# The state scan of an S5 layer: from one block split between VectorE and GpSimd to pieces set between the gates' matrix products, all on VectorE

## The chip, the cores and the metric

The kernel runs on one core of a Trainium2 chip. The metric is the device time of one execution in microseconds (us); the time of a kernel is the median of several runs. A core has a matrix engine (PE, with its weight loads shown apart as PEld), a vector engine (DVE, VectorE), an activation engine (ACT, ScalarE), a general engine (POOL, GpSimd) and a queue that issues transfers (SP). Each engine works through its own instructions in an order that is fixed when the program is built.

## The reference, cut to what matters

The program is a two-layer decoder trunk of width 1024 over 2048 tokens. Its even layer has two branches; the change lies in branch B, a diagonal state space model with 32 groups of 16 channels and a complex state of 64 numbers for each group:

```python
proj = h @ even_w_in[i]
q, k, v, z_a, u, z_b = jnp.split(proj, [...], axis=-1)
o_a = stick_breaking_attention(q, k, v) * jax.nn.silu(z_a)
o_b = s5_mixer(u, ...) * jax.nn.silu(z_b)
x = x + jnp.concatenate([o_a, o_b], axis=-1) @ even_w_out[i]

def s5_mixer(u, ...):
    bu = einsum('gnp,blgp->blgn', b_bar, uf)                  # complex
    h  = associative_scan over time of  h_t = lam_bar * h_{t-1} + bu_t
    y  = Re(einsum('gpn,blgn->blgp', c, h)) + d_skip * uf
    y  = gelu(y);  return y * sigmoid(y @ w_glu + b_glu)
```

## The kernel before, in words

**Stages of the even layer.** `tile_trunk` (line 1233) calls in this order: `first_gates` and a first `gates` (half of z_a), `s5_in` (line 1278: the input u, its products with B, and the scan), a second `gates` (line 1279: the other half of z_a), `s5_out` (line 1280: the outputs from the state), a third `gates` (line 1283: z_b), then the GLU and the attention.

**The state.** Time is cut into 256 columns of eight tokens (`NC` = 256), so the recurrence runs over columns. The state tile has 128 partitions (a pair of groups, 64 states each), sixteen pairs, real and imaginary part, and 256 columns after one column of zeros. Before the change there are two such tiles, `H[0]` and `H[1]`, of eight pairs each, with the parts outermost: `[P, 2, 8, 257]`.

**`s5_in` (line 465).** For each half `cb` of the channels and each half of the time it makes eight products `j` of 24 matmuls (L67 to L69, tile `ups`): the activations hT, taken at every eighth token, are split into a rounded part on ACT (`sh`, L314) and a remainder on DVE (`sl`, L315). ACT copies the result to `U` (L487). Then four groups of transposes (`tp`, L491), ACT copies (`us`, L493) and products with B (`bp`, L500) follow, and DVE copies each `bp` into H (L504).

**The scan.** The scan over columns is a tree. `scan_up` (line 510) combines, for four pairs at a time, neighbouring columns at distance 1 (level 0, in two halves), 2 (level 1) and 4 (level 2) on DVE, and then walks a chain over every eighth column on POOL: 31 links of four small instructions for each tile (L530 to L533). `scan_down` (line 536) hands the results back through levels 2, 1 and 0 on DVE. One level step is `cplx_acc` (line 450), five DVE instructions: a product with the real factor into `ca` (L458), two products with the imaginary factor into `cb` (L460), their sum (L461) and the sum onto H (L462). The factors are `pwr` and `pwi`, made in `s5_setup` (line 213) by repeated squaring, one set for each level. `ca`, `cb` and the chain's `sa`, `sb` lie in the pools of `s5_in`, on the same side of the memory on which `s5_out` opens its own pools later.

**`gates` (line 420).** It loads eight pieces of a weight (split into `whi` on ACT and `wlo` on DVE) and, for each of four blocks `m` of 512 tokens, splits the activations (four `sh` on ACT, four `sl` on DVE), runs 96 matmuls into four accumulators `gps`, and hands them out (`silu_out`: a sigmoid on ACT, L364, a product on DVE, L365, a store). The four accumulators are reused from block to block, so a block can begin in an accumulator only when DVE's product L365 has read the one before. For `m` = 0 and 3 the loop over the weight's pieces is outermost; for 1 and 2 the loop over the four output slices is.

**`s5_out` (line 549).** For each quarter `ct` of the pairs it loads K0, Co and U, multiplies H by Co (L570) and U by K0 (L573) into `yps`, and makes the gelu on ACT and DVE (L577 to L582).

**What sets the order.** Nobody writes the order of an engine's queue by hand here. A scheduler (asked for in line 1370) plays the program through and gives each engine, whenever it is free, the instruction that comes first in the program text among those whose inputs and buffers are there. A piece of work that comes earlier in the text goes first wherever it is ready, and later work fills the gaps. The order it finds is then fixed, and on the chip an engine that reaches an instruction whose input is missing waits, with all that stands behind it.

Of the kernel before, what the change touches and what calls it, by code (L numbers as in the profile page):

```python
# [9 lines left out]
F32 = mybir.dt.float32  # L10
F32R = mybir.dt.float32r
BF16 = mybir.dt.bfloat16
AF = mybir.ActivationFunctionType
ALU = mybir.AluOpType
# [3 lines left out]
P = 128  # L18
L = 2048
D = 1024  # L20
# [92 lines left out]
NI = 16  # L113
NC = L // T8
# [41 lines left out]
def s5_setup(e, room, lr, li, dt, sn, sh, b_re, b_im, c_re, c_im, dsk, bin_d, k0_d, co_d):  # L156
# [10 lines left out]
    e.pwr = [e.cst.tile([P, NI], F32, name=f"pwr{a}") for a in range(4)]  # L167
    e.pwi = [e.cst.tile([P, 2, NI], F32, name=f"pwi{a}") for a in range(4)]
    with e.pool("s5s", 1, "right") as s, e.pool("s5t", 2, "right") as s2, e.pool("s5w", 1, "right") as sw, \
# [43 lines left out]
        for a in range(6):  # L213
# [206 lines left out]
def gates(e, pn, hT, w, c0, out_d, row0, lo_eng, between=None, also=None, ws=None, sp=None, last=LAST):  # L420
# [5 lines left out]
    for m in range(4):  # L426
# [11 lines left out]
        for f, k in order:  # L438
            wh, wl = ws[k]
            hi, lo = sp[k // 2]  # L440
            c = slice(f * P, f * P + P)
            i = mm3(nc, pss[f], wh[:, c], wl[:, c], hi[:, k % 2], lo[:, k % 2], k == 0,
                    k == (last[-1] if m == 3 else KD - 1))
# [6 lines left out]
def cplx_acc(e, tp, dst, src, lv, n, eng):  # L450

    nI = dst.shape[2]
    i0 = e.i0
# [10 lines left out]

def s5_in(e, pn, hT, w_in, bin_d, u_d, H, lo_eng):

    nc, tc = e.nc, e.tc
    with e.pool("u_b", 2, "right") as ub, e.pool("u_1", 1, "right") as u1, e.pool("u_p", 2, "right", PSUM) as up:
        ws = pn.load(w_in, 4 * D, 512, lo_eng)
        for cb in range(2):  # L470
            nc.vector.memset(H[cb][:, :, :, 0:1], 0.0)
# [3 lines left out]
            for half in range(2):  # L475
                U = ub.tile([P, 16, T8, 16], F32, tag="U", name="U")
                for j in range(T8):
# [9 lines left out]
                    nc.scalar.activation(U[:, :, j, :], ps.rearrange("c (g p) -> c g p", p=16), AF.Copy)  # L487
                for g4 in range(4):
# [14 lines left out]
                    i0 = g4 * 2  # L503
                    nc.vector.tensor_copy(H[cb][:, :, i0:i0 + 2, 1 + half * P:1 + (half + 1) * P], bp)  # L504
            scan_up(e, H[cb], cb * 8, u1, ub)
        for cb in range(2):
            scan_down(e, H[cb], cb * 8, u1)


def scan_up(e, H, i1, tp, t2):  # L510

    B = H[:, :, :, 1:]
    V, G = e.nc.vector, e.nc.gpsimd
    for i0 in range(0, 8, 4):
        e.i0 = i1 + i0
        b = B[:, :, i0:i0 + 4]
        for h in range(2):
            c = slice(h * 128, h * 128 + 128)
            bh = b[:, :, :, c]
            cplx_acc(e, tp, bh[:, :, :, 1::2], bh[:, :, :, 0::2], 0, 64, V)  # L520
        cplx_acc(e, tp, b[:, :, :, 3::4], b[:, :, :, 1::4], 1, 64, V)
        cplx_acc(e, tp, b[:, :, :, 7::8], b[:, :, :, 3::8], 2, 32, V)
    ii = slice(i1, i1 + 8)
    pr = e.pwr[3][:, ii].unsqueeze(1).to_broadcast([P, 2, 8])
    pi = e.pwi[3][:, :, ii]
    for c in range(15, NC, 8):
        src = B[:, :, :, c - 8]
        a = t2.tile([P, 2, 8], F32, tag="sa", name="sa")
        b = t2.tile([P, 2, 8], F32, tag="sb", name="sb")
        G.tensor_tensor(a, src, pr, ALU.mult)  # L530
        G.tensor_tensor(b, src[:, ::-1], pi, ALU.mult)
        G.tensor_tensor(a, a, b, ALU.add)
        G.tensor_tensor(B[:, :, :, c], B[:, :, :, c], a, ALU.add)  # L533


def scan_down(e, H, i1, tp):

    B = H[:, :, :, 1:]
    V = e.nc.vector
    for i0 in range(0, 8, 4):  # L540
        e.i0 = i1 + i0
        b = B[:, :, i0:i0 + 4]
        cplx_acc(e, tp, b[:, :, :, 11::8], b[:, :, :, 7:NC - 1:8], 2, 31, V)
        cplx_acc(e, tp, b[:, :, :, 5::4], b[:, :, :, 3:NC - 1:4], 1, 63, V)
        cplx_acc(e, tp, b[:, :, :, 2:128:2], b[:, :, :, 1:127:2], 0, 63, V)
        cplx_acc(e, tp, b[:, :, :, 128::2], b[:, :, :, 127:NC - 1:2], 0, 64, V)
# [827 lines left out]
```

## Time and profile before

| | |
|---|---|
| median of 3 runs | 2875.68 us (2871.69 to 2877.24) |
| the profiled execution, its own time | 2872.48 us |
| its span, first to last instruction | 2870.8 us |
| PE busy | 2765.3 us (96%) |
| DVE busy | 1719.9 us (60%) |
| ACT busy | 1365.0 us (48%) |
| POOL busy | 1197.6 us (42%) |
| mean granted clock of PE | 0.989 |

Shares of the whole span say little about a stage that takes a tenth of it. In the stage of the scan, from about 227 to 417 us of the span, DVE is the busiest engine beside PE, and the questions are where PE stands idle and what it waits for. The profile names for every idle stretch the instruction that ended it ("[16.98 <-DVE sg L365]"), and the timeline of the engine named shows what stood ahead of that instruction.

### The profile page before, as it was taken

To read this page: it belongs to the slowest core of one execution; us is meant where nothing else is said; L and a number is where in the kernel's file an instruction comes from. 1 tells how busy PE (TensorE), PEld (TensorE's weight loads), DVE (VectorE), ACT (ScalarE), POOL (GpSimd) and SP (SyncE) were. 2 spreads that over 40 slices of the span, in tenths; PEclk is the share of its full clock that TensorE was granted. 3 is DMA by queue.
4 is the path that set the end of the run, shared out by engine and by line. 5 is a ranking of instruction groups with operands and counts; after the bars stand their busy time and mean duration, and the time that the engine had idled before them with its cause. 6 is when DMAs were issued, how large, how long until landed. Compare 5 with 4: busy or idle time off the path is not lost.

```text
span 2870.8 us, 46525 instructions
## 1 busy us (share of the span) xinstructions
PE 2765.3 (96%) x17433; PEld 2496.6 (87%) x17433; DVE 1719.9 (60%) x2733; ACT 1365.0 (48%) x2988; POOL 1197.6 (42%) x1321
## 2 busy tenths in 40 slices
PE   6989979899999999999999999999999999999999
PEld 6788767889999999999899978887788999999887
DVE  7768965657676857685767783223345566565521
ACT  4576224446555655555555552223345566565310
POOL 7201821366665665666556730000023455455300
PEclk9999989999999999999999999999999999999999
DMA  5532136511110111111112124332131021121343
GB/s 170 153 81 75 58 94 201 173 44 43 29 41 27 45 29 40 29 41 27 41 27 73 58 72 143 104 103 86 56 99 41 31 67 54 36 78 60 125 137 114
DMA packets 246898, 215.69 MB, mean 75 GB/s; under 512 B 46256, under 2 KB 215568, under 8 KB 246160
## 3 DMA queue, kind: packets, MB, share of 16 engines
q1 hardware_dynamic: 246096, 210.62, 24.2%
q8 instruction: 137, 2.24, 0.3%
q10 hardware_dynamic: 576, 2.10, 0.2%
q14 instruction: 89, 0.73, 0.1%
HBM read 129.36 MB, written 74.65 MB: 71 GB/s over the span
## 4 chain that ended last, share of the span: by engine, by line
PE 78%; DVE 7%; POOL 4%; issue 4%; ACT 3%; DMA 3%; SPq 1%; ACTq 0%; POOLq 0%; DVEq 0%
PE av L807 6%; PE pp L68 6%; PE pp L67 6%; PE pp L69 6%; PE ops L69 5%; PE ops L68 5%; PE ops L67 5%; PE w L796 4%; PE gps L67 3%; PE gps L68 3%; PE gps L69 3%; PE qk L67 2%; PE qk L69 2%; PE qk L68 2%; PE z L68 2%
## 5 line engine op out<-in xcount | busy, mean ns | idle before, releaser
L719 POOL TENSOR_TENSOR sl<-hT,sh 128x1024 fp32r<-128x1024 f32 x128 | 322.2, 2518 | 343.0 <-ACT sh L718 304.8
L67 PE MATMUL pp<-whi,sh 128*128 128x384 f32 x1024 | 357.4, 349 | 0.7 <-ACT whi L314 0.6
L68 PE MATMUL pp<-wlo,sh 128*128 128x384 f32 x1024 | 351.1, 343 | 0.2
L69 PE MATMUL pp<-whi,sl 128*128 128x384 f32 x1024 | 348.0, 340 | 0.0
L790 DVE TENSOR_TENSOR_SCAN pt<-om,pt,zero 128x513 f32<-128x513 f32 x192 | 279.2, 1477 | 38.0 <-ACT om L788 37.3
L67 PE MATMUL gps<-sh,whi 128*128 128x512 f32 (+1 forms) x672 | 252.8, 389 | 23.1 <-DVE sg L365 20.3
L68 PE MATMUL gps<-sl,whi 128*128 128x512 f32 (+1 forms) x672 | 259.1, 386 | 3.5 <-DVE sl L315 3.5
L69 PE MATMUL gps<-sh,wlo 128*128 128x512 f32 (+1 forms) x672 | 256.5, 384 | 0.0
L799 DVE TENSOR_TENSOR tl<-w,th 128x512 fp32r<-128x512 f32 (+2 forms) x320 | 186.6, 599 | 95.5 <-ACT th L798 93.6
L798 ACT ACTIVATE th<-w 128x512 fp32r<-128x512 f32 (+2 forms) x320 | 163.9, 535 | 149.3 <-PE w L796 148.8
L315 DVE TENSOR_TENSOR sl<-hT,sh 128x1024 fp32r<-128x1024 f32 (+1 forms) x148 | 172.1, 1186 | 50.4 <-ACT sh L314 48.2
L69 PE MATMUL ops<-woh,ol 128*128 128x512 f32 x496 | 196.8, 397 | 0.7 <-DVE ol L315 0.7
L68 PEld LDWEIGHTS pp<-wlo,sh 128*128 128x128 f32 x1024 | 193.6, 189 | 3.8 <-POOL wlo L315 1.7
L67 PEld LDWEIGHTS pp<-whi,sh 128*128 128x128 f32 x1024 | 193.5, 189 | 3.6 <-ACT whi L314 1.3
L68 PE MATMUL ops<-wol,oh 128*128 128x512 f32 x496 | 196.2, 395 | 0.0
L67 PE MATMUL ops<-woh,oh 128*128 128x512 f32 x496 | 195.6, 395 | 0.0
L69 PEld LDWEIGHTS pp<-whi,sl 128*128 128x128 f32 x1024 | 193.3, 189 | 2.6
L790 DVE TENSOR_TENSOR_SCAN pt<-om,zero 128x129 f32<-128x129 f32 (+3 forms) x128 | 158.8, 1262 | 56.8 <-ACT om L788 56.2
L314 ACT ACTIVATE sh<-hT 128x1024 fp32r<-128x1024 f32 (+1 forms) x148 | 155.8, 1093 | 62.0 <-PE gps L69 32.5
L788 ACT ACTIVATE om<-z 128x512 f32<-128x512 f32 (+2 forms) x320 | 167.0, 538 | 37.6 <-PE z L784 22.7
L718 ACT ACTIVATE sh<-hT 128x1024 fp32r<-128x1024 f32 x128 | 135.5, 1059 | 90.8 <-PE pp L68 90.5
L796 PE MATMUL w<-ident,pt 128*128 128x128 f32 x1088 | 165.2, 273 | 8.6 <-DVE tl L799 6.0
(327 smaller groups left out, 8001.7 us busy)
## 6 DMA issues: line engine op xcount, KB each, us to landing
zs_d<-sg SPq DMA_DIRECT2D x80, 256.0 KB
o<-o_d SPq DMA_DIRECT2D x80, 256.0 KB
xt<-in_x_dram SPq DMA_DIRECT2D x28, 512.0 KB
r<-in_even_w_in_dram SPq DMA_DIRECT2D x64, 192.0 KB
zs<-zs_d SPq DMA_DIRECT2D x64, 128.0 KB
o_d<-ot SPq DMA_DIRECT2D x64, 128.0 KB
r<-in_odd_w_in_dram SPq DMA_DIRECT2D x64, 128.0 KB
zs<-zs_d SPq DMA_DIRECT2D x32, 256.0 KB
```

Source lines behind the costliest of these rows:

```text
L67: nc.tensor.matmul(out, lhsT=lhi, rhs=rhi, start=start, stop=False)
L68: nc.tensor.matmul(out, lhsT=lhi, rhs=rlo, start=False, stop=False)
L69: return nc.tensor.matmul(out, lhsT=llo, rhs=rhi, start=False, stop=stop)
L314: a = nc.scalar.activation(hi, src, AF.Copy)
L315: b = lo_eng.tensor_tensor(lo, src, hi.bitcast(F32), ALU.subtract)
L719: a = nc.gpsimd.tensor_tensor(sl, ht, sh.bitcast(F32), ALU.subtract)
L788: nc.scalar.activation(o[:, lo:512], z[:, :n], AF.Sigmoid, scale=-scale)
L790: nc.vector.tensor_tensor_scan(pt[:, lo:][:, ::-1], o[:, lo:][:, ::-1], zr.to_broadcast([P, n + 1]), 1.0 if prev[i] is None else prev[i], ...
L796: nc.tensor.transpose(w[:, s, :], pt[:, lo + s * P:lo + (s + 1) * P], e.ident)
L798: nc.scalar.activation(th[:, :ni, qs], w[:, :ni, :], AF.Copy)
L799: nc.vector.tensor_tensor(tl[:, :ni, qs], w[:, :ni, :], th[:, :ni, qs].bitcast(F32), ALU.subtract)
L807: nc.tensor.matmul(av[:, qs], lhsT=a[:, s, :], rhs=b[:, s, qs], start=diag and x == 0, stop=c == 0 and x == len(prods) - 1)
```

## The change

The arithmetic of the tree stays, but its last step up, its order and its engines change:

- One tile H holds all sixteen pairs, with the pair outermost: `[P, 16, 2, 257]`. ACT, not DVE, copies `bp` into it.
- The tree gets one more level (distance 8, level 3) in both directions, so the chain runs over every sixteenth column: 15 links instead of 31, each over all sixteen pairs at once, four instructions of 128x32 on DVE instead of POOL. One more power of the factor is made for it (seven squarings instead of six, 5 sets of `pwr` and `pwi`).
- Levels 0 and 1 are made pair by pair with fused instructions (`cplx_pair`): one `scalar_tensor_tensor` for the product with the real factor and its sum onto H, and one each for the two parts of the product with the imaginary factor, three instructions of one pair over all its columns and without temporary tiles. Levels 2 and 3 keep `cplx_acc`, over eight pairs at once.
- The scan becomes a list of pieces. A piece is one pair of level 0 or 1, one `cplx_acc`, or one link. `s5_in` runs one piece behind every product `j`; as the list is empty during the first half of the channels, that is 16 of the 18 pieces up of the first eight pairs, during the second half. What is left (2 + 18 pieces up, 15 links, 36 pieces down) is run from the second `gates`, in front of every eighth product of three matmuls, that is four times for each block `m`: six pieces each time, four within the chain. By the counts that gives 24 pieces in block 0 (2 + 18 up and 4 links), 18 in block 1 (11 links, 7 down), 24 in block 2 (all down) and the last 5 in block 3.
- The temporary tiles lie in a pool of their own (`Ht`); the pool of `y` in `s5_out` has two buffers instead of three.

```diff
@@ s5_setup
-    e.pwr = [e.cst.tile([P, NI], F32, name=f"pwr{a}") for a in range(4)]
-    e.pwi = [e.cst.tile([P, 2, NI], F32, name=f"pwi{a}") for a in range(4)]
+    e.pwr = [e.cst.tile([P, NI], F32, name=f"pwr{a}") for a in range(5)]
+    e.pwi = [e.cst.tile([P, 2, NI], F32, name=f"pwi{a}") for a in range(5)]
...
-        for a in range(6):
+        for a in range(7):
@@ gates
-        for f, k in order:
+        for n, (f, k) in enumerate(order):
+            if slot is not None and n % 8 == 7:
+                slot(m, n // 8)
@@
+def cplx_pair(e, dst, src, lv, i):
+
+    V, MU, AD = e.nc.vector, ALU.mult, ALU.add
+    V.scalar_tensor_tensor(dst, src, e.pwr[lv][:, i:i + 1], dst, MU, AD)
+    for r in range(2):
+        V.scalar_tensor_tensor(dst[:, r], src[:, 1 - r], e.pwi[lv][:, r, i:i + 1], dst[:, r], MU, AD)
+
+class Scan:
+    def __init__(self, e, H, tp):
+        self.e, self.H, self.tp, self.todo = e, H, tp, []
+
+    def level(self, cb, lv, dst, src):
+        B = self.H.rearrange("p i r c -> p r i c")[:, :, :, 1:]
+        if lv < 2:
+            for i in range(cb * 8, cb * 8 + 8):
+                self.todo.append(lambda i=i: cplx_pair(self.e, B[:, :, i, dst], B[:, :, i, src], lv, i))
+        else:
+            i0, i = cb * 8, slice(cb * 8, cb * 8 + 8)
+            self.todo.append(lambda: cplx_acc(self.e, self.tp, B[:, :, i, dst], B[:, :, i, src], lv, i0,
+                                              self.e.nc.vector))
+
+    def up(self, cb):
+        for lv in range(4):
+            s = 2 << lv
+            self.level(cb, lv, slice(s - 1, NC, s), slice(s // 2 - 1, NC, s))
+
+    def down(self, cb):
+        for lv in range(3, -1, -1):
+            s = 2 << lv
+            self.level(cb, lv, slice(s + s // 2 - 1, NC, s), slice(s - 1, NC - 1, s))
+
+    def chain(self):
+        self.todo += [lambda c=c: self.link(c) for c in range(31, NC, 16)]
+
+    def link(self, c):
+        e, B, G = self.e, self.H.rearrange("p i r c -> p r i c")[:, :, :, 1:], self.e.nc.vector
+        src = B[:, :, :, c - 16]
+        a = self.tp.tile([P, 2, NI], F32, tag="sa", name="sa")
+        b = self.tp.tile([P, 2, NI], F32, tag="sb", name="sb")
+        G.tensor_tensor(a, src, e.pwr[4].unsqueeze(1).to_broadcast([P, 2, NI]), ALU.mult)
+        G.tensor_tensor(b, src[:, ::-1], e.pwi[4], ALU.mult)
+        G.tensor_tensor(a, a, b, ALU.add)
+        G.tensor_tensor(B[:, :, :, c], B[:, :, :, c], a, ALU.add)
+
+    def run(self, n):
+        for f in self.todo[:n]:
+            f()
+        del self.todo[:n]
@@ s5_in
                     nc.scalar.activation(U[:, :, j, :], ps.rearrange("c (g p) -> c g p", p=16), AF.Copy)
+                    sc.run(1)
...
-                    nc.vector.tensor_copy(H[cb][:, :, i0:i0 + 2, 1 + half * P:1 + (half + 1) * P], bp)
-            scan_up(e, H[cb], cb * 8, u1, ub)
-        for cb in range(2):
-            scan_down(e, H[cb], cb * 8, u1)
+                    i0 = cb * 8 + g4 * 2
+                    nc.scalar.activation(H[:, i0:i0 + 2, :, 1 + half * P:1 + (half + 1) * P],
+                                         bp.rearrange("p a i c -> p i a c"), AF.Copy)
+            sc.up(cb)
@@ s5_out
-    ... e.pool("so_3", 3, "right") as s3
+    ... e.pool("so_3", 2, "right") as s3
...
-                                             rhs=H[ct // 2][q, a, ct % 2 * 4 + i, 0:NC], start=a == 0, stop=False)
+                                             rhs=H[q, ct * 4 + i, a, 0:NC], start=a == 0, stop=False)
@@ tile_trunk
-        H = [hpool.tile([P, 2, 8, NC + 1], F32, name=f"H{cb}") for cb in range(2)]
-        s5_in(e, pn, hT, w0, bin_d, u_d, H, V)
-        gates(e, pn, hT, w0, 3 * D + 512, zs_d, 512, V)
+        H = hpool.tile([P, NI, 2, NC + 1], F32, name="H")
+        scan = Scan(e, H, sr.enter_context(e.pool("Ht", 1, "right")))
+        s5_in(e, pn, hT, w0, bin_d, u_d, H, scan, V)
+        n_up = len(scan.todo)
+        scan.chain()
+        n_chain = len(scan.todo) - n_up
+        scan.down(0)
+        scan.down(1)
+
+        def slot(m, i):
+            scan.run(4 if n_down < len(scan.todo) <= n_down + n_chain else 6)
+
+        n_down = len(scan.todo) - n_up - n_chain
+        gates(e, pn, hT, w0, 3 * D + 512, zs_d, 512, V, slot=slot)
+        scan.run(len(scan.todo))
         s5_out(e, H, u_d, k0_d, co_d, y_d)
```

More of the change, by code (lines that the diff above doesn't have):

```diff
@@ L417, in first_gates, with gates @@
     return ws, angles, rows[:, 3]
-def gates(e, pn, hT, w, c0, out_d, row0, lo_eng, between=None, also=None, ws=None, sp=None, last=LAST):
+def gates(e, pn, hT, w, c0, out_d, row0, lo_eng, between=None, also=None, ws=None, sp=None, last=LAST,
+          slot=None):
     nc = e.nc
@@ L447, in gates, with cplx_acc @@
     return out
-def cplx_acc(e, tp, dst, src, lv, n, eng):
-    nI = dst.shape[2]
-    i0 = e.i0
+def cplx_acc(e, tp, dst, src, lv, i0, eng):
+    nI, n = dst.shape[2:]
     a = tp.tile([P, 2, nI, n], F32, tag="ca", name="ca")
@@ L462, in cplx_acc, with s5_in @@
     eng.tensor_tensor(dst, dst, a, ALU.add)
-def s5_in(e, pn, hT, w_in, bin_d, u_d, H, lo_eng):
+def cplx_pair(e, dst, src, lv, i):
[38 more added lines that the diff above has]
+        del self.todo[:n]
+def s5_in(e, pn, hT, w_in, bin_d, u_d, H, sc, lo_eng):
     nc, tc = e.nc, e.tc
@@ L469, in s5_in @@
         ws = pn.load(w_in, 4 * D, 512, lo_eng)
+        nc.vector.memset(H[:, :, :, 0:1], 0.0)
         for cb in range(2):
-            nc.vector.memset(H[cb][:, :, :, 0:1], 0.0)
             bt = u1.tile([P, 2, 8, P], F32, tag="bt", name="bt")
@@ L502, in s5_in @@
                                                  rhs=us[:, i * 2 + par, :], start=True, stop=True)
-                    i0 = g4 * 2
-                    nc.vector.tensor_copy(H[cb][:, :, i0:i0 + 2, 1 + half * P:1 + (half + 1) * P], bp)
-            scan_up(e, H[cb], cb * 8, u1, ub)
-        for cb in range(2):
-            scan_down(e, H[cb], cb * 8, u1)
[L510 to L546, printed above, removed]
+                    i0 = cb * 8 + g4 * 2
+                    nc.scalar.activation(H[:, i0:i0 + 2, :, 1 + half * P:1 + (half + 1) * P],
+                                         bp.rearrange("p a i c -> p i a c"), AF.Copy)
+            sc.up(cb)
 def s5_out(e, H, u_d, k0_d, co_d, y_d):
@@ L552, in s5_out @@
     V, A = nc.vector, nc.scalar
-    with e.pool("so_1", 1, "right") as s1, e.pool("so_2", 2, "right") as s2, e.pool("so_3", 3, "right") as s3, \
+    with e.pool("so_1", 1, "right") as s1, e.pool("so_2", 2, "right") as s2, e.pool("so_3", 2, "right") as s3, \
             e.pool("so_p", 2, "right", PSUM) as pp:
```

## The prediction, made before the changed kernel ran

> **What bounds the kernel now.** I read the page first: PE is busy for 96% of the span, so only PE's idle stretches and its slowed stretches can be won. Then the busy time by stages around the scan:
>
> ```profile
> core 0: us, PE busy (x) PEld busy (x) DVE busy (x) ACT busy (x) POOL busy (x), PEclk, DMA share, GB/s
> 227.00:256.00 29.00, 26.37 (x236) 25.86 (x235) 28.80 (x42) 22.47 (x28) 0.00 (x0) 0.99 0.26 73
> 256.00:270.00 14.00, 11.88 (x99) 11.58 (x100) 13.97 (x21) 3.99 (x6) 0.00 (x0) 0.78 0.01 1
> 270.00:298.00 28.00, 28.00 (x201) 24.14 (x200) 17.25 (x22) 12.47 (x20) 23.12 (x65) 1.00 0.38 114
> 298.00:348.00 50.00, 50.00 (x221) 40.90 (x219) 49.13 (x82) 16.44 (x22) 43.42 (x95) 1.00 0.14 53
> 348.00:366.00 18.00, 14.15 (x54) 11.00 (x54) 17.76 (x25) 4.38 (x6) 16.45 (x26) 0.91 0.24 74
> 366.00:382.00 16.00, 11.16 (x57) 8.78 (x55) 0.00 (x0) 4.77 (x7) 12.61 (x59) 0.99 0.18 50
> 382.00:417.00 35.00, 22.86 (x91) 18.80 (x92) 33.76 (x55) 6.56 (x8) 1.78 (x6) 0.76 0.26 84
> 417.00:500.00 83.00, 82.19 (x401) 62.35 (x401) 45.46 (x67) 38.74 (x62) 13.67 (x10) 1.00 0.62 190
> ```
>
> DVE is full wherever the scan runs, except from 366 to 382, where it does nothing while POOL works. The timelines of PE and DVE say what ended PE's idle time and what stood ahead of that:
>
> ```profile
> 258.12 3.70 PE L500 MATMUL bp<-us,bt 128*64 128x128 f32 x32 [4.75 <-DVE H L504]
> 294.62 2.02 PE L500 MATMUL bp<-us,bt 128*64 128x128 f32 x32
> 351.14 0.79 PE L68 MATMUL gps<-sl,whi 128*128 128x512 f32 x1 [3.14 <-DVE sl L315]
> 353.86 1.10 PE L67 MATMUL gps<-sh,whi 128*128 128x512 f32 x3
> 355.67 0.50 PE L67 MATMUL gps<-sh,whi 128*128 128x512 f32 x1 [0.71 <-DVE sg L365]
> 394.14 0.80 PE L67 MATMUL gps<-sh,whi 128*128 128x512 f32 x1 [16.98 <-DVE sg L365]
> 398.88 0.39 PE L69 MATMUL gps<-sh,wlo 128*128 128x512 f32 x1
> ```
>
> ```profile
> 382.39 0.59 DVE L458 TENSOR_TENSOR ca<-H,pwr 128x248 f32<-128x248 f32 x1 [16.54 <-POOL H L533]
> 393.40 1.28 DVE L365 TENSOR_TENSOR sg<-sg,gps 128x512 f32<-128x512 f32 x2
> ```
>
> At 365.9 DVE reaches the first step down of the second tile and waits 16.54 us for POOL's chain. Behind it stand the products L365 that free PE's accumulators, so PE stands still for 16.98 us. The other gaps come from DVE as well: copies into H and remainders `sl` that are late behind scan steps. Idle time: 4.75 + 3.14 + 0.71 + 16.98 = 25.6 us. After each gap PE runs slower for a while: 11 matmuls from 394.14 to 398.88 take 4.74 us where 221 in 50.00 us make 0.226 each (2.2 us lost), nine from 351.14 to 354.96 lose 1.8 by the same pace, and the 32 `bp` take 3.70 instead of 2.02 us (1.7). Sum: **31.3 us** at stake, no more. After 394 PE has no gap worth counting in the rows down to 500 us, so what is won earlier moves everything after it.
>
> **The change part by part.** (1) *POOL's chain goes.* With it go the 16.54 us, for certain; what is late next is DVE, so its work has to be added up. (2) *DVE's steps.* One run of the old steps, almost undisturbed:
>
> ```profile
> 327.03 1.22 DVE L315 TENSOR_TENSOR sl<-hT,sh 128x1024 fp32r<-128x1024 f32 x1
> 328.16 0.45 DVE L461 TENSOR_TENSOR ca<-ca,cb 128x256 f32<-128x256 f32 x1
> 329.69 0.68 DVE L365 TENSOR_TENSOR sg<-sg,gps 128x512 f32<-128x512 f32 x1
> 330.29 0.66 DVE L462 TENSOR_TENSOR H<-H,ca 128x256 f32<-128x256 f32 x1
> 330.86 0.67 DVE L460 TENSOR_TENSOR cb<-H,pwi 128x124 f32<-128x124 f32 x2
> 331.46 1.20 DVE L315 TENSOR_TENSOR sl<-hT,sh 128x1024 fp32r<-128x1024 f32 x1
> 332.59 0.61 DVE L458 TENSOR_TENSOR ca<-H,pwr 128x248 f32<-128x248 f32 x1
> 334.38 1.04 DVE L458 TENSOR_TENSOR ca<-H,pwr 128x504 f32<-128x504 f32 x1
> 335.34 1.10 DVE L460 TENSOR_TENSOR cb<-H,pwi 128x252 f32<-128x252 f32 x2
> 336.48 0.73 DVE L461 TENSOR_TENSOR ca<-ca,cb 128x504 f32<-128x504 f32 x1
> 338.35 0.69 DVE L458 TENSOR_TENSOR ca<-H,pwr 128x504 f32<-128x504 f32 x1
> 338.95 0.81 DVE L460 TENSOR_TENSOR cb<-H,pwi 128x252 f32<-128x252 f32 x2
> 340.40 0.68 DVE L365 TENSOR_TENSOR sg<-sg,gps 128x512 f32<-128x512 f32 x1
> 340.99 0.68 DVE L462 TENSOR_TENSOR H<-H,ca 128x504 f32<-128x504 f32 x1
> 341.59 0.81 DVE L460 TENSOR_TENSOR cb<-H,pwi 128x256 f32<-128x256 f32 x2
> ```
>
> From start to start, four pairs cost 3.97 us at level 1 (334.38 to 338.35), 2.65 for a half of level 0 (338.35 to 341.59 without the 0.59 of `sg`), and 2.39 at level 2 (0.60 + 1.79). So the old scan costs 8 x (3.97 + 5.30 + 2.39) = 93.3 us of DVE, and the 16 copies L504 some 0.6 each (the `sg` of the same size), 9.6 more, that go to ACT.
>
> The new steps: an instruction of n elements costs 0.076 us + 1.04 ns x n (from 504 in 0.60 and 1024 in 1.13 us). At level 1, where elements lie four words apart, `ca` takes 0.96 us for 504: 1.75 ns each. A fused pair has 256 + 128 + 128 elements at level 0: 0.76 us; at level 1 128 + 64 + 64: 0.68 us. Where an instruction needs the one before it, the next starts later (336.48 is 1.14 after 335.34, for two that need 0.52 each; 0.1 or so). I take 0.80 us for any fused pair: 64 x 0.80 = 51.2. Four `cplx_acc` at level 2 have twice the pairs and half the columns of an old level 1: 4 x 3.97 = 15.9; four at level 3 cost 4 x 2.39 = 9.6. A link is four instructions, three in a row:
>
> ```profile
> L173 DVE TENSOR_TENSOR f<-f,f x2: 165/165/165, 34.0 to 34.1; 128x16 f32<-128x16 f32 x2
> L958 DVE SCALAR_TENSOR_TENSOR h<-xt,ors,ogb x16: 1277/1284/1287, 1735.6 to 2007.3; 128x1024 f32<-128x1024 f32 x16
> L493 ACT ACTIVATE us<-tp x16: 578/598/654, 187.2 to 290.3; 128x512 f32<-128x512 f32 x16
> ```
>
> The first of these rows gives 0.6 to 1.0 us for a link, depending on how much 32 scattered elements cost beyond 16; I take 0.75, near the row: 15 x 0.75 = 11.3. New scan: 51.2 + 15.9 + 9.6 + 11.3 = 88.0 us against 102.9 with the copies: DVE is relieved by 15 us.
>
> What the trace does not show is a fused step with both inputs strided. If the second stream costs nothing more, a level-1 pair takes 0.68 us; if it adds its full surcharge of 0.71 ns per element again, 0.86; without any surcharge, 0.50. The middle is what I use. The second row above bears on whether fusing itself is slow: 1024 elements with both inputs in the same memory take 1.28 us, as long as the plain subtraction `sl` of 1024 (1.22), so one element per step of 1.04 ns. The Trainium skill, "Vector Engine (DVE) Microarchitecture Reference", section 7 "Points that are easy to get wrong", says the opposite: a scalar-tensor-tensor instruction with two sources in SBUF that are not bf16 runs at half the throughput. By that rule the fused pairs would cost some 34 us more in all, an estimate; the L958 row disagrees with it.
>
> *Does DVE keep up?* Its busy times from 227 to 417 add up to 160.7 us. Less the old scan and the eight copies that lie there (93.3 + 4.8), with the new scan: 150.6. From 270 to 298 it had 10.75 us without work, because the second half's products were not there; two `cplx_acc` pieces of the first half (6.4) now fall into that, 4.4 stay idle. So the scan ends near 227 + 150.6 + 4.4 = 382 instead of at 416.6 (the last L462 starts at 415.95): 34.6 us sooner, while PE is at most 31.3 us sooner. Against PE's work the scan stands no later than before, and before, PE had no gap beside its end. DVE has the room, with 3 us to spare; the question is the order.
>
> (3) *The order.* Block m of `gates` takes PE 96 x 0.226 = 21.7 us. DVE owes each block four `sl` (1.13 each) and four `sg` (0.60), 6.9 us, and its pieces: block 0: 16 fused, two `cplx_acc`, four links, 22.2 (the other two pieces lie earlier, above); block 1: 11 links, two `cplx_acc`, five fused, 18.7; block 2: 22 fused and two `cplx_acc`, 24.0; block 3: five fused, 4.0, and eight `wlo` of 0.6. Together 29.1, 25.6, 30.9 and 15.7 us: in three blocks more than PE needs, by 7.4, 3.9 and 9.2. Since the pieces of a block precede the next block's `sl` in the text, they go first wherever they are ready. In the rows above the `sl` slip in between steps of one `cplx_acc` (328.54 between two that depend on each other). Links and `cplx_acc` still leave such gaps; eight fused pairs are independent and leave none, 6.4 us in which no `sl` gets through. Such runs can meet the ends of blocks 0 and 2; the serial stretches (16 us of `cplx_acc` and links behind the steps up) cover the end of block 1. PE can also begin a block with the two of three products that do not need `sl`, as in the row of 353.86. So between 0 and 12.8 us of new waits; I take **6**.
>
> (4) *Copies on ACT.* One takes 0.6 us there (the L493 row): 16 x 0.6 = 9.6 us; in the half-period from 227 to 256 ACT is busy 22.47 of 29 us and gets 2.4 more. What hides it is this slack; where a copy queues behind an `sh` that waits for PE, the two `bp` buffers hold PE up. Between 0 and 9.6; I take **1.5**, as ACT's slack is larger than the addition. (5) *The rest.* A seventh squaring adds seven instructions of 0.165 us at about 55 us of the span, where only the scan needs them: 0, at most 1.2. The second `y` buffer less: DVE is busy 45.46 of 83 us from 417 to 500, so a wait there is covered: 0, at most 3. Earlier loads for `s5_out`: nothing, as PE is busy 82.19 of those 83 us.
>
> **The sum.** 31.3 - 6 - 1.5 = 23.8 us. The profiled execution took 2872.48 us, so 2848.7 for its like; the median of the runs is 3.2 us higher, and I predict **2852**. About 0.2% (5.8 us) is what a measurement of this kernel can tell from no change.
>
> **The rivals.** *Strict order:* the scheduler puts all pieces of a block ahead of the next block's `sl`, and PE pays the whole excess, 20.5 us instead of 6. For it: the text's order and the independence of the pairs; against it: the `sl` between the rows above. 31.3 - 20.5 - 1.5 = 9.3, that is 2866. *Strict order and dear steps, slower:* the same place, the ends of blocks 0 to 2, where 43 fused pieces stand ahead of the remainders. If a fused step takes a second 1.04 ns for each element (512 to a pair at level 0: 0.53 us more), the excess is 20.5 + 43 x 0.53 = 43.3, more than the 31.3 won: 13.5 us slower, 2889. It decides from 29.8 - 20.5 = 9.3 us over 43 pieces on, 0.22 each, a pair of 1.02 us. The L958 row speaks against it, the unseen strides for it. (The page's rule of half the throughput, above, would bring this about.) *ACT becomes the bound of `s5_in`:* copies late by their full 9.6: 31.3 - 6 - 9.6 = 15.7, 2860. *The hole stays:* chain and levels on DVE take as long as POOL's chain did; the 88.0 against 102.9 speak against that; it is the point between the first two rivals, at about 2876.
>
> **How the numbers follow.** The forecast (waits of 0 to 12.8) gets 0.55, with 2845 to 2859; ACT as the bound 0.07; strict order 0.18; the point of no change 0.10; slower 0.10. Faster by over 0.2%: 0.55 + 0.07 + 0.18 = 0.80; within: 0.10; slower: 0.10. For the range: no new waits at all and no cost on ACT give 2844, runs of the kernel before lie up to 4 us under their median, so from 2841; up to strict order with a few us beyond, 2871.
>
> **What would show it.** Right: no instruction on POOL between 227 and 417; no idle time of DVE of over 5 us with the scan unfinished; the 16.98 us gap gone; fused steps of 256 and 128 elements at 0.34 and 0.21 us from start to start at level 0; the scan done by about 382. Wrong: PE gaps that DVE's `sl` ends at the starts of blocks 1 and 3, 20 us together (strict order); fused pairs of over 1.0 us (dear steps); gaps before `bp` or `ups` that ACT ends (copies).

## The result, and the profile after

The changed kernel takes 2850.68 us (median of three runs, 2848.27 to 2854.24), the kernel before 2874.44 in the same comparison: a ratio of 0.9919, 95% interval 0.9899 to 0.9938. The forecast was 2852. The profiled execution took 2848.27 us, with a span of 2846.6 us and a mean granted clock of 0.992. Three executions were disturbed and took two to three and a half times as long, a fourth of the changed kernel, the profiled one of e3 below and one of the kernel before in a later comparison; they are left out, and with its fourth run the changed kernel's median would be 2852.46.

The busy time by stages around the scan, of the kernel after (columns: stretch, its length, then busy time and instructions of PE, PEld, DVE, ACT and POOL, granted clock, DMA share, GB/s):

```profile
227.00:256.00 29.00, 29.00 (x272) 28.19 (x272) 28.93 (x54) 24.57 (x32) 0.00 (x0) 1.00 0.24 70
256.00:270.00 14.00, 14.00 (x111) 13.67 (x111) 11.16 (x12) 9.48 (x14) 0.00 (x0) 1.00 0.05 14
270.00:298.00 28.00, 26.55 (x171) 21.67 (x170) 21.87 (x55) 12.72 (x19) 0.00 (x0) 1.00 0.64 191
298.00:348.00 50.00, 47.04 (x205) 38.00 (x204) 48.59 (x143) 14.26 (x18) 0.00 (x0) 0.97 0.18 64
348.00:366.00 18.00, 18.00 (x78) 13.03 (x77) 18.00 (x40) 5.16 (x9) 0.00 (x0) 0.90 0.28 87
366.00:382.00 16.00, 16.00 (x78) 12.40 (x76) 16.00 (x46) 8.78 (x13) 0.00 (x0) 1.00 0.48 150
382.00:417.00 35.00, 32.61 (x152) 24.15 (x152) 22.85 (x36) 12.92 (x21) 0.00 (x0) 0.95 0.59 183
```

POOL does nothing there any more, DVE works through from 298 to 382 without the 16 idle us, and PE is short of 1.5, 3.0 and 2.4 us in three of the stretches, where before it was short of 2.6, 2.1, 3.9, 4.8 and 12.1 in five. What is left shows in the timeline of PE, after:

```profile
297.59 0.50 PE L67 MATMUL gps<-sh,whi 128*128 128x512 f32 x1 [1.45 <-DVE sg L365]
343.43 0.51 PE L67 MATMUL gps<-sh,whi 128*128 128x512 f32 x1 [1.58 <-DVE sg L365]
345.32 2.08 PE L588 MATMUL yps<-H,Co 64*128 64x256 f32 x8 [1.38 <-issue]
347.33 2.07 PE L591 MATMUL yps<-U,K 128*128 128x256 f32 x4
385.08 0.50 PE L67 MATMUL gps<-sh,whi 128*128 128x512 f32 x1 [2.01 <-DVE sg L365]
386.06 0.63 PE L67 MATMUL gps<-sh,whi 128*128 128x512 f32 x1
386.49 0.63 PE L68 MATMUL gps<-sl,whi 128*128 128x512 f32 x1
407.12 1.10 PE L591 MATMUL yps<-U,K 128*128 128x256 f32 x4 [0.38 <-DMA U<-u_d]
```

Three waits for the product `sg` and one for which the profile names no releaser ("issue"; in e2 below it names DVE's H at the same place), 1.45 + 1.58 + 1.38 + 2.01 = 6.4 us. Behind two of these places PE runs slowly: four `yps` in 2.07 us where the same four take 1.10 at 407, and matmuls 0.43 us apart (386.06 to 386.49) where 0.226 is the normal pace.

For an account, one interval is enough: from the first product of `s5_in` (`ups`) to the first transpose of the attention behind the branch (tile `w`). Before, then after (columns: shortest, median and longest duration in ns, first and last start in us):

```profile
L67 PE MATMUL ups<-whi,sh x256: 277/283/583, 150.0 to 275.3; 128*128 128x256 f32 x128
L796 PE MATMUL w<-ident,pt x1088: 269/272/334, 608.9 to 1705.1; 128*128 128x128 f32 x182
```

```profile
L67 PE MATMUL ups<-whi,sh x256: 278/283/493, 150.0 to 267.7; 128*128 128x256 f32 x128
L814 PE MATMUL w<-ident,pt x1088: 270/272/330, 587.8 to 1686.1; 128*128 128x128 f32 x182
```

The interval, called the scan interval below, shrinks from 458.9 to 437.8 us: **21.1 us**. The spans differ by 24.2. So some 3 us of the gain in the profiles lie behind the scan, in stages that the change doesn't touch. The clearest of them is the linear attention of the second layer; its products `pv`, before and after:

```profile
L67 PE MATMUL pv<-gwh,gsh x512: 274/281/288, 2173.8 to 2682.1; 128*128 128x256 f32 x171
```

```profile
L67 PE MATMUL pv<-gwh,gsh x512: 276/276/286, 2155.2 to 2658.9; 128*128 128x256 f32 x171
```

The median falls from 281 to 276 ns, and this stretch from 508.3 to 503.7 us. The other stages behind the scan give back part of that. Why the same matmul is 5 ns shorter in the changed program was not tried.

The fused steps, the links and the end of the scan, in DVE's timeline after:

```profile
221.65 1.63 DVE L470 SCALAR_TENSOR_TENSOR H<-H,pwr 128x256 f32<-128x256 f32 x4
223.18 2.15 DVE L472 SCALAR_TENSOR_TENSOR H<-H,pwi 128x128 f32<-128x128 f32 x8
...
309.04 0.22 DVE L511 TENSOR_TENSOR sa<-H,pwr 128x32 f32<-128x32 f32 x1
309.18 0.20 DVE L512 TENSOR_TENSOR sb<-H,pwi 128x32 f32<-128x32 f32 x1
309.41 0.19 DVE L513 TENSOR_TENSOR sa<-sa,sb 128x32 f32<-128x32 f32 x1
309.64 0.22 DVE L514 TENSOR_TENSOR H<-H,sa 128x32 f32<-128x32 f32 x1
309.89 0.21 DVE L511 TENSOR_TENSOR sa<-H,pwr 128x32 f32<-128x32 f32 x1
...
332.98 2.94 DVE L470 SCALAR_TENSOR_TENSOR H<-H,pwr 128x126 f32<-128x126 f32 x8
337.37 3.51 DVE L472 SCALAR_TENSOR_TENSOR H<-H,pwi 128x63 f32<-128x63 f32 x14
375.49 4.28 DVE L472 SCALAR_TENSOR_TENSOR H<-H,pwi 128x127 f32<-128x127 f32 x16
379.69 1.27 DVE L597 TENSOR_TENSOR sq<-sq,yps 128x512 f32<-128x512 f32 x2
```

At level 0 a fused instruction of 256 elements takes 0.38 us from start to start (four in 1.53), one of 128 elements 0.25 to 0.27: a pair costs 0.89 to 0.92 us. At level 1, 126 elements take 0.35 and 63 elements 0.24: some 0.84. A link takes 0.85 (309.04 to 309.89). The scan ends at 379.7.

### The profile page after: what moved, and what is told of

It is laid out like the page before. It is cut to its first block, busy times and chain, and to the rows that moved or that the text cites. A ratio compares the mean times of both kernels' runs of the same rounds, so it can differ in the third digit from the quotient of the medians.

```text
span 2846.6 us, 46385 instructions
## 1 busy us (share of the span) xinstructions
PE 2763.5 (97%) x17433; PEld 2493.8 (88%) x17433; DVE 1710.8 (60%) x2855; ACT 1375.1 (48%) x3004; POOL 1103.3 (39%) x1073
## 4 chain that ended last, share of the span: by engine, by line
PE 79%; DVE 8%; POOL 3%; issue 3%; ACT 3%; DMA 2%; SPq 1%; ACTq 0%; POOLq 0%; DVEq 0%
PE av L825 6%; PE pp L67 6%; PE pp L68 6%; PE pp L69 5%; PE ops L69 5%; PE ops L67 5%; PE ops L68 5%; PE w L814 4%; PE gps L67 4%; PE gps L68 3%; PE gps L69 3%; PE qk L67 2%; PE qk L69 2%; PE qk L68 2%; PE z L67 2%
## 5 line engine op out<-in xcount | busy, mean ns | idle before, releaser
L315 POOL TENSOR_TENSOR wlo<-r,whi 128x384 fp32r<-128x384 f32 x64 | 75.4, 1193 | 335.6 <-ACT whi L314 329.8
```

What stands on the lines that cost most here:

```text
L315: b = lo_eng.tensor_tensor(lo, src, hi.bitcast(F32), ALU.subtract)
```

## The experiments

All were compared with the kernel before, whose median lay between 2872.70 and 2875.48 us in the four comparisons; so the ratios can be set beside each other, the medians only roughly. The scan interval is that of the profiled execution. Three executions of one and the same program (after, after_again and, as will be seen, e1) give 437.8, 436.9 and 437.4 us, so I take a difference of over 2 us in the interval for one of the kernel. Of the kernel before there is one profile, and its own scatter is not known.

| kernel | scan interval, us | median, us | ratio to before, 95% interval |
|---|---|---|---|
| before | 458.9 | 2874.44 | 1 |
| e7: before, chains on DVE | 456.4 | 2874.23 | 0.9986 to 1.0009 |
| f1: before, copies on ACT | 452.6 | 2871.59 | 0.9985 to 1.0003 |
| f2: before, both | 457.1 | 2876.99 | 1.0004 to 1.0023 |
| after | 437.8 | 2850.68 | 0.9899 to 0.9938 |
| after_again: the same | 436.9 | 2848.48 | 0.9892 to 0.9926 |
| e1: after, scan in one block | 437.4 | 2849.47 | 0.9894 to 0.9927 |
| e2: after, links on POOL | 439.7 | 2849.74 | 0.9897 to 0.9927 |
| e3: after, no fused steps | no profile | 2854.08 | 0.9910 to 0.9943 |
| e4: after, copies on DVE | 448.5 | 2859.44 | 0.9929 to 0.9959 |
| e5: after, four pieces a place | 438.8 | 2849.97 | 0.9896 to 0.9928 |
| e6: after, 64 more steps | 435.0 | 2850.60 | 0.9897 to 0.9929 |
| f3: after, no fused steps, links on POOL | 445.9 | 2855.82 | 0.9930 to 0.9955 |
| f4: after, 31 links on POOL | 445.8 | 2855.63 | 0.9932 to 0.9959 |

**e1, the whole rest of the scan ahead of the gates, the places between the products unused.**

```diff
-        gates(e, pn, hT, w0, 3 * D + 512, zs_d, 512, V, slot=slot)
-        scan.run(len(scan.todo))
+        scan.run(len(scan.todo))
+        gates(e, pn, hT, w0, 3 * D + 512, zs_d, 512, V)
```

> The changed kernel, but what is left of the scan after s5_in stands in the text as one block ahead of the second gates, so every piece goes before every remainder sl and every product sg of those gates where it is ready. The work on each engine is the same. Measured by the start of the first attention transpose on PE (608.9 us in the kernel before, 587.8 in the changed one), which takes in the whole stage and nothing behind it. If the order counts (dense fused pieces hold up the remainders): PE waits of 10 us or more in blocks 1 to 3 and the mark at 598 to 610. If only the sum of DVE's work counts: the mark within 3 us of 587.8.

Measured: no difference, and the reason is plain. The instructions of all five engines stand in exactly the same order in both programs. The scheduler fills the queues with what is ready; pieces set six at a time between the products come early enough to be taken at the same moments as pieces set in one block. That the pieces stand between the gates' products is thus no change of the program at all, and e1 is one more measurement of after.

**e5, four pieces at each place instead of six.**

```diff
-            scan.run(4 if n_down < len(scan.todo) <= n_down + n_chain else 6)
+            scan.run(4)
```

> The changed kernel with four pieces at each of the 16 places instead of six (four in the chain already), the last seven pieces behind the second gates, ahead of s5_out. Block 0 then has 16 pieces instead of 24. If the gaps of the changed kernel (1.45 us at the start of block 1, 1.58 and 1.38 at 343 to 345, 2.01 at 385, all ended by DVE's product sg, and about 4.7 us of slow pace behind them) come from too many pieces ahead of sg: they shrink, the mark (start of the first attention transpose, 587.8) at 582 to 586. If the pieces only move the gap to s5_out and the third gates: 587 to 592.

Measured: 438.8 us and the same time. Here the order on DVE and PE does differ a little, from about 348 us on: the wait at 385 us is gone, and others came, the largest of 2.36 us for the load of Co at 379. That is the second expectation.

**e2, the fifteen links on POOL.**

```diff
-        e, B, G = self.e, self.H..., self.e.nc.vector
+        e, B, G = self.e, self.H..., self.e.nc.gpsimd
```

> The changed kernel with the 15 links on POOL again, four instructions each as before. A link took 1.09 us on POOL in the quiet part of the trace of before (368 to 382 us) and 1.65 on the mean of the second chain, so 16 to 25 us for 15 links, in which DVE has only remainders and products sg to do (about 10 us). If the wait of DVE for POOL was the main cause of the lost time: an idle stretch of DVE of 8 to 15 us before the steps down, PE gaps that follow from it, the mark (587.8) at 593 to 600. If the fused steps and the placing are what brought the gain: the mark within 3 us.

Measured: 2 to 3 us more in the interval, no difference in the time. DVE's timeline shows its wait for the chain, and PE's what followed:

```profile
308.23 0.69 DVE L365 TENSOR_TENSOR sg<-sg,gps 128x512 f32<-128x512 f32 x1 [1.18 <-ACT sg L364]
313.67 0.69 DVE L365 TENSOR_TENSOR sg<-sg,gps 128x512 f32<-128x512 f32 x1 [4.75 <-ACT sg L364]
315.55 3.94 DVE L315 TENSOR_TENSOR sl<-hT,sh 128x1024 fp32r<-128x1024 f32 x3 [1.20 <-ACT sh L314]
...
328.06 0.58 DVE L460 TENSOR_TENSOR ca<-H,pwr 128x240 f32<-128x240 f32 x1 [6.78 <-POOL H L514]
```

```profile
344.83 0.79 PE L67 MATMUL gps<-sh,whi 128*128 128x512 f32 x1 [4.41 <-DVE sg L365]
```

The chain needs some 23 us on POOL for its 15 links (the first starts at 306.6, the last at 328.1), 1.5 us each, against 0.85 on DVE. Meanwhile DVE has the gates' own work and idles 13.9 us in four stretches, the last of 6.78. PE then waits 4.41 us for `sg` where after waits 1.58 (1.51 and 1.52 in its repeats). So where a short chain runs does show at PE, but it matters little in the time.

**e3, levels 0 and 1 with `cplx_acc` over two and four pairs instead of fused steps.**

```diff
-            for i in range(cb * 8, cb * 8 + 8):
-                self.todo.append(lambda i=i: cplx_pair(...))
+            g = 2 << lv
+            for i in range(cb * 8, cb * 8 + 8, g):
+                self.todo.append(lambda: cplx_acc(..., pairs i to i + g, lv, i, DVE))
+                self.todo += [lambda: None] * (g - 1)
```

> The changed kernel with levels 0 and 1 in the five unfused instructions again (two pairs at level 0, four at level 1 to a step of 512 elements), the same places in the text. DVE's steps: level 0 costs 1.32 us for a pair instead of 0.92, level 1 0.99 instead of 0.87: 32 x 0.40 + 32 x 0.12 = 16.6 us more on DVE; but these steps wait for each other, so remainders get in between. If DVE's sum binds: scan done 16 us later and the mark (587.8) at 600 to 606. If waits at the block ends bind: more gaps for the remainders make up for it, the mark at 586 to 594.

Measured: 2854.08. The intervals of the ratios overlap with those of after; but in the same comparison all three runs (2853.78 to 2855.03) lie above all four of e1 (2847.83 to 2852.09), which is the same program as after. On the mean they are 4.6 us longer, so the fused steps are worth about that. There is no undisturbed profile of e3, so where the time goes, and which expectation holds, stays open.

**e4, the copies back on DVE.**

```diff
-                    nc.scalar.activation(H[...], bp..., AF.Copy)
+                    nc.vector.tensor_copy(H[...], bp...)
```

> The changed kernel with the 16 copies into H on DVE again (0.6 us each, 9.6 in all, eight of them after 227 us). If the gap of 4.75 us before bp came from DVE being full with the old steps alone: no PE gap over 1 us in s5_in and the mark (587.8) within 3 us. If the move of the copies to ACT is what closed it: a PE gap of 3 to 5 us before bp that DVE's copy ends, with the slow pace behind it, the mark at 592 to 595.

Measured: 10.7 us more in the interval than after, 2859.44, more than either expectation. The old gap is back, and more of it, in PE's timeline of e4:

```profile
258.47 3.71 PE L558 MATMUL bp<-us,bt 128*64 128x128 f32 x32 [6.13 <-DVE H L562]
395.17 0.80 PE L67 MATMUL gps<-sh,whi 128*128 128x512 f32 x1 [4.36 <-DVE sg L365]
```

6.13 us of waiting for the copy plus 1.7 of slow pace (3.71 against 2.02); the rest lies in larger waits at the gates, mostly for `sg`, 9.8 us against 6.4; that they grow because DVE has the copies to do as well is likely, but not shown apart.

**e6, one more DVE instruction of 128 elements behind each fused pair.**

```diff
+    V.tensor_tensor(e.dm[:, 1], e.dm[:, 0], e.dm[:, 0], AD)
```

> The changed kernel with one more DVE instruction of 128 elements behind each fused pair, on a scratch tile that nobody reads: 0.2 to 0.25 us for each of 64 pairs, 13 to 16 us of DVE in all, 9 to 11 of them in the pieces ahead of the remainders of blocks 1 to 3. If the pieces hold PE up by their full time (strict order): the mark (587.8) at 597 to 602 and the slow pace on top. If DVE carries the backlog into the next stage and PE sees only a part: 588 to 594.

Measured: no difference in the time and an interval of 435.0 us, 1.9 to 2.8 less than the three of after, for which no cause was sought. The run doesn't test what it was meant to. The added instructions depend on nothing, and the scheduler moved all 64 ahead of the scan:

```profile
L473 DVE TENSOR_TENSOR dm<-dm x64: 268/292/339, 143.8 to 199.6; 128x128 f32<-128x128 f32 x64
```

What dearer fused steps would do stays open from this run; their price is read from the profile of after instead.

**after_again, the changed kernel in a later comparison.**

> The changed kernel once more, for how far its stage repeats from profile to profile: the mark at 587.8 within 1 us, the gaps at 297, 343 to 345 and 385 us in the same places; the whole span may differ by 3 us for reasons behind the stage.

Measured: 2848.48 and 436.9 us, the size of the scatter used above. The waits are in the same places, at 299, 345, 347 and 387 us, and the first three nearly as long as in after, but the last is 3.18 us instead of 2.01, and no slow pace follows it:

```profile
386.50 0.50 PE L67 MATMUL gps<-sh,whi 128*128 128x512 f32 x1 [3.18 <-DVE sg L365]
386.83 0.39 PE L68 MATMUL gps<-sl,whi 128*128 128x512 f32 x1
387.06 0.40 PE L69 MATMUL gps<-sh,wlo 128*128 128x512 f32 x1
```

**e7, the kernel before with both chains of 31 links on DVE.**

```diff
-    V, G = e.nc.vector, e.nc.gpsimd
+    V, G = e.nc.vector, e.nc.vector
```

> The kernel before with nothing changed but the engine of its two chains of 31 links: DVE instead of POOL. A link on DVE takes 0.85 us in the changed kernel (309.04 to 309.89), so 62 links put 53 us on DVE and take its wait of 16.5 us for POOL away. If DVE's room decides: slower than before, the mark (608.9) at 620 to 645. If the hop to POOL and back is what costs: the mark at 592 to 600.

Measured: nothing won, although the hole of 16.98 us is gone (the wait at the same place is 0.67 us). DVE now has 62 links of some 0.74 us, 46 us more, and its last scan step starts at 434.74 us instead of 415.95. The outputs `yps` run 20 us later, to 499.4 instead of 479.8, and in the stage behind them PE lacks work. In PE's timeline of e7, and then of before, which has one wait there as well:

```profile
509.39 0.66 PE L67 MATMUL pp<-whi,sh 128*128 128x384 f32 x1 [1.85 <-DVE y L582]
519.30 0.62 PE L67 MATMUL pp<-whi,sh 128*128 128x384 f32 x2 [2.92 <-ACT whi L314]
532.96 0.58 PE L67 MATMUL gps<-hi,gwh 128*128 128x256 f32 x1 [8.32 <-ACT gwh L314]
```

```profile
532.50 0.58 PE L67 MATMUL gps<-hi,gwh 128*128 128x256 f32 x1 [6.33 <-DVE sg L365]
```

From 500 to 540 PE is busy 24.17 us at a granted clock of 0.74, where before it was 32.91 at 0.87. So 8.7 us of new idle time here, 3.3 in two new waits at 279 and 426 us and the slower pace take back most of what closing the hole had won: of 16.3 us, 2.5 are left in the interval.

**f1, the kernel before with the copies on ACT.**

```diff
-                    nc.vector.tensor_copy(H[cb][...], bp)
+                    nc.scalar.activation(H[cb][...], bp, AF.Copy)
```

> The kernel before with one part of the change: the sixteen copies into H on ACT instead of DVE, the scan untouched. Theory A (the parts add up, and the copies are worth what their return to DVE cost, some 10 us): the 4.75 us gap before bp is gone, the two chains on POOL start some 6 to 9 us sooner, and the first attention transpose starts at 598 to 601 us instead of 608.9; median about 2864. Theory B (the gain at bp only lengthens the hole, because POOL's chains set the end of the scan): the hole grows from 16.98 to 20 us or more, the transpose starts at 605 to 609, median 2871 to 2875.

Measured: in the interval 6.3 us less, close to what stood at `bp` (4.75 of waiting, 1.7 of slow pace). The wait there is gone (a new one of 1.80 us, for `sl`, stands at 269 us), the hole stays as it was:

```profile
253.84 2.02 PE L500 MATMUL bp<-us,bt 128*64 128x128 f32 x32
391.73 0.79 PE L67 MATMUL gps<-sh,whi 128*128 128x512 f32 x1 [16.93 <-DVE sg L365]
```

So neither theory as it was put: the hole doesn't grow, and the copies are worth 6 us, not 10, as long as the rest is old. In the whole time nothing of it can be told from no change (2871.59 against 2872.70). In the profiled execution some 5 us are lost again behind the interval, 4.0 of them in the stretch of the `pv` matmuls (512.3 against 508.3 us), and for what reason stays open.

**f2, the kernel before with both.**

```diff
  both edits of e7 and f1
```

> The kernel before with two parts: the copies on ACT and both chains of 31 links on DVE. Moving the chains alone closed the hole but won nothing, since 62 links of 0.75 us made DVE's scan end at 434.7 instead of 416 and the time came back as waits between 500 and 533 us. Theory A (DVE's sum decides when the scan ends): 16 copies of 0.6 us less and bp some 6 us sooner, so the scan ends at 419 to 426 and the transpose starts at 595 to 600. Theory B (the waits at 500 to 533 come from the order in which weights are loaded, not from the scan's end): they stay, and the transpose starts at 602 to 608.

Measured: 457.1 us, and slower than before by 1 to 7 us (ratio 1.0004 to 1.0023). Theory A fails: DVE's last scan step starts at 434.5 as in e7, not at 419 to 426, and the transpose at 608.9. That is close to the 602 to 608 of theory B, and PE waits between 500 and 540 us (busy 25.05 at a clock of 0.72). But as the scan ends as late as in e7, the run can't say whether those waits come from its end or, as theory B has it, from the order of the loads.

**f3, after without fused steps and with its links on POOL.** The edits of e3 and e2 together.

> The changed kernel without its fused steps (levels 0 and 1 in three-operation steps over two and four pairs) and with its fifteen links on POOL; what remains of the change is the level more, the single short chain over all sixteen pairs and the copies on ACT. Theory A (the short single chain and the copies are the change; fusing and the engine of the chain are of no weight): the transpose starts at 588 to 594, median 2849 to 2856. Theory B (each of the two takes a reserve that the other leaves, so that both together uncover a wait): 598 or later, median over 2860, with a PE gap of 5 us or more that DVE ends between 340 and 400 us.

Measured: 445.9 us and 2855.82. Theory A fails on the interval: the two edits together cost 8 us. In PE's timeline of f3 stands a wait as theory B asked for:

```profile
347.16 0.80 PE L67 MATMUL gps<-sh,whi 128*128 128x512 f32 x1 [5.38 <-DVE sg L365]
354.75 0.50 PE L67 MATMUL gps<-sh,whi 128*128 128x512 f32 x1 [1.65 <-DVE sg L365]
```

But e2 has 4.41 us at this place, with the links on POOL alone, and the total stays under the 2860 of theory B. Another 4.3 us of waiting stands in `s5_out` (2.38 at 417 us for the load of U, 1.96 at 432 for `y`). Against e2, which differs by the fused steps alone, f3 has 6.2 us more of interval. Even so, this kernel is 13 us of interval better than before: the extra level, one chain for both halves, the copies on ACT and the new layout and pools carry most of the change, together.

**f4, after without the extra level: one chain of 31 links, on POOL.**

```diff
-        for lv in range(4):            # up; range(3, -1, -1) down
+        for lv in range(3):            # up; range(2, -1, -1) down
-    range(31, NC, 16), c - 16, pwr[4], pwi[4], nc.vector
+    range(15, NC, 8),  c - 8,  pwr[3], pwi[3], nc.gpsimd
```

> The changed kernel without its extra level: one chain of 31 links over all sixteen pairs, on POOL; fused steps and copies on ACT stay. Against the fifteen links on POOL (DVE idle 6.8 us for them, and no loss in time) it has 16 links more at some 1.4 us, 22 us, and DVE has two level-3 pieces less on either side. Theory A (the length of the serial chain decides): DVE idles some 30 us, a PE gap of 10 to 20 us stands again where DVE's products wait behind the scan, and the transpose starts at 600 to 608. Theory B (one chain instead of two is enough): within 4 us of the changed kernel, 586 to 593.

Measured: 445.8 us and 2855.63, between the theories. Against e2, which differs by the extra level alone, that is 6.1 us more of interval. DVE does idle as theory A says, in the stretch table and the timeline of DVE in f4:

```profile
298.00:348.00 50.00, 46.93 (x207) 38.51 (x206) 21.18 (x28) 14.88 (x19) 35.91 (x115) 1.00 0.19 69
```

```profile
349.61 1.04 DVE L460 TENSOR_TENSOR ca<-H,pwr 128x496 f32<-128x496 f32 x1 [6.64 <-POOL H L514]
```

But PE waits only 7.92 us (at 352.85, for `sl`) plus 2.16 (at 459.46), and from 298 to 348 it is busy 46.93 of 50 us: while POOL walks the chain, DVE serves the gates. So of the 24 us by which the chain on POOL is longer than in e2, a quarter reaches the interval.

## Why the prediction was right, point by point

- **What was at stake, 31.3 us.** All of it went: the waits of 4.75, 3.14, 0.71 and 16.98 us are gone from the places where they stood. A further 1.0 us went at about 167 us, where a wait for `U` of 2.15 us became two of 0.5 together: the first `bp` starts at 188.4 instead of 189.4. That was not forecast.
- **New waits, 6 forecast.** 6.4 measured, at 297, 343, 345 and 385 us; in after_again it is 7.6. As the 6 was taken from near the middle of a range from 0 to 12.8, that it came so close is luck. The place was partly other than thought: not the remainders `sl` at the start of a block, but the product `sg` behind runs of fused steps: the wait of 1.58 us ends with an `sg` that DVE starts at 342.67, behind the fourteen steps L472 of 337.37 and four more.
- **The step that was left out: the slow pace behind new waits.** The prediction counted it for the waits that went (5.7 us) and not for those that came. From 345.32 to 351.66 us eight and four `yps` and six matmuls take 6.34 us, where the `yps` take 1.06 us each time when fast and the six 1.36: 2.9 us lost. From 385.65 to 389.05 eight matmuls take 3.40 instead of 1.81 us, 1.6 lost: together 4.5 us. This term differs from one execution to the next: in after_again, with the same program, it is about 1.5 us, none of it behind the wait of 3.18. The Trainium skill, "TensorE: Matmul & The Clock Gate", Part 1, gives half the clock after idle windows and 427 ns from start to start for 512 columns when slow; the 0.43 us here agree. Its idle window of about 3.4 us is longer than the single wait of 2.01 us, behind which the slow pace began half a microsecond later. So the length of the wait just before does not tell in these traces whether a slow stretch follows.
- **Copies on ACT, 1.5 forecast.** Nothing is seen: no wait of PE for ACT between 170 and 295 us, and the last `ups` starts 7.6 us sooner, which is about the 6.4 at `bp` and the 1.0 above.
- **The sum.** 31.3 + 1.0 - 6.4 - 4.5 = 21.4 us against 21.1 measured in the interval. The forecast was 23.8, too much by 2.7. The total came out within 1.3 us of the forecast because a further 3 us appeared behind the interval, which the prediction didn't know of. That much of the agreement is chance.
- **DVE's steps.** The end of the scan was forecast at 382 and came at 379.7, but the prices behind it were off in both directions. A fused pair costs 0.89 to 0.92 and 0.84 us instead of 0.80, a link 0.85 instead of 0.75. Added up from start to start in the two traces, the new scan takes DVE 90.3 us and the old one 89.7, or 100.0 with its copies: DVE is relieved by 9.7 us and not by 15, and by the copies alone. DVE did not have less idle time either: it is busy 142.25 of the 152.7 us from 227 to 379.7, so it idles 10.4 us where 4.4 were forecast. What made up for it lies at the edges: 5.8 us of fused steps ran before 227 us, and 5.0 us less of DVE's other work than was counted lay before the scan's end. The slope of a fused step is 1.0 ns per element at level 0 (0.38 for 256, 0.25 for 128) and 1.75 at level 1, as the prediction had them; the fixed part is 0.13 us instead of 0.076. The Trainium skill's rule of half throughput for such instructions ("Vector Engine (DVE) Microarchitecture Reference", section 7) doesn't show in these rows: at half rate 256 elements would take over 0.53 us, an estimate from twice the slope of 1.04 ns.
- **The rival of strict order.** Waits at the ends of the blocks did come, 6.4 us and not 20.5. That the text order of the pieces against the gates was not what decides is shown by e1: with all pieces ahead of every `sl` the queues are the same.
- **The rival of dear steps, slower.** Its point was a pair of 1.02 us together with strict order; 0.92 at level 0 is under it, though not by much. No run raised the price (e6 didn't), so how near the point was is only argued.
- **What the change says, against what it does.** The prediction took every part as working. Taken alone in the old kernel, chains on DVE win nothing (e7) and copies 6 us of interval (f1); together they win nothing either (f2). What makes DVE able to carry the chain is probably its length: 15 links over all pairs, 12.8 us, instead of 62 links, 46 us; a long chain on DVE in the new kernel was not tried, but on POOL the extra level is worth 6.1 us (f4 against e2). The links on DVE are worth 2 to 3 us of interval (e2), the fused steps about 4.6 us of time (e3); without both, the interval is 8 us longer (f3). By its ratio f3 costs 7 to 10 us of time, where e2 costs nothing that can be told and e3 4.6. So the links on DVE and the fused steps may in part be each other's reserve, but without a profile of e3 that is not shown.

**A part that was never undone.** The prediction put the earlier loads for `s5_out` at nothing. Before, the scan's temporary tiles lay where `s5_out` opens its pools, K0 is loaded only when the scan is over (its last step starts at 415.95), and the products of U with K0 follow at 423.8, long after the first products of H with Co at 375.2. After, both run from 345 to 347 us on, between the gates' products, with the scan still going. The load in SyncE's timeline of before, then the products before and after:

```profile
416.67 1.00 SPq L557 DMA_DIRECT2D K<-k_d  x2
```

```profile
L573 PE MATMUL yps<-U,K x64: 378/379/484, 423.8 to 479.8; 128*128 128x256 f32 x64
```

```profile
L591 PE MATMUL yps<-U,K x64: 378/379/793, 347.3 to 430.5; 128*128 128x256 f32 x64
```

The four kernels with the old pools have intervals of 452.6 us and more, all with the new ones that have a profile 448.5 or less. No run changes the pools alone, so how much of the gain is theirs stays open.

No variant beats the changed kernel: e1, e2, e5 and e6 are its equals, and the simplest of them is e1, which emits the scan in one block.

## What to carry to other kernels

When a wait is removed, ask what the engine that now works instead of waiting will be late with: e7 closed a hole of 17 us and lost most of it again within 140 us, because the work had only changed places. Shorten the serial part first (a level more, one chain for all); then its engine hardly matters. Where a scheduler sets the order, compare the queues before believing that a new place in the text does anything, and when you cost new waits of PE, allow for slow matmuls behind them, as a range. A total that agrees with the forecast proves little until the parts have been added up as well.

## What the runs showed of the hardware that was not expected

- A fused instruction with strided data has a fixed part of 0.13 us (0.38 and 0.25 us for 256 and 128 elements, 0.35 and 0.24 for 126 and 63), nearly twice the 0.076 us of plain ones. Whether fusing or the stride makes it was not separated.
- A link of four small dependent instructions takes 1.5 us on POOL (e2) and 0.85 on DVE at 32 elements, although one such instruction is only 0.27 against 0.21 us.
- The same `pv` matmuls, in the same stage with the same text, have a median of 281 ns in the kernel before, e7, f1 and f2, and of 276 or 277 in the changed kernel and all its variants that have a profile. Their stretch takes 508.3 to 512.3 us in the first four and 502.3 to 504.6 in the others, so some 4 us or more of a kernel's time hang on this alone, and no run here shows the cause.
- The same wait of PE for `sg` has eight slow matmuls behind it in after (2.01 us long) and e1 (1.91), and none in after_again (3.18).
